# Hybrid decoder block: new leads for two products' weight slabs, their low parts by transfer in the mixers, and no forming jobs at the last convolution output

## The chip, the cores and the metric

The kernel runs on one core of a Trainium2 chip. The metric is the device time of one execution in microseconds (us); the time before is the median of three runs. In the text PE is TensorE, DVE is VectorE, ACT is ScalarE, POOL is GpSimd and SP is SyncE, as the profile names them.

## The reference

One decoder layer on x of 512 tokens by 1024 features, in float32:

```python
h = h + 0.5 * swiglu(rms_norm(h, g_ffn1), w_ffn1_gate, w_ffn1_up, w_ffn1_down)   # D_FF = 2816
z = rms_norm(h, g_mix) @ w_in                 # conv GLU | q | k | v | merge-gate logits
y_conv = conformer_conv(a_glu, w_dw, b_dw, g_conv_ln, b_conv_ln, w_conv_out)     # width 31
y_attn = o.reshape(b, s, ATTN_OUT_W) @ w_attn_out      # dilated windowed attention, 12 heads
h = h + (g_a * y_conv + g_b * y_attn) @ w_mix_out
h = h + 0.5 * swiglu(rms_norm(h, g_ffn2), w_ffn2_gate, w_ffn2_up, w_ffn2_down)
h = h + sigmoid(rms_norm(h, g_ple) @ w_ple_gate) * (p @ w_ple_proj)
return rms_norm(h, g_final)
```

swiglu(x, g, u, d) is (silu(x @ g) * (x @ u)) @ d. The change touches the product with w_mix_out ("mixers") and, through a shared table, the weights of both FFNs.

## The kernel before, in words

**Numbers in two parts.** Every matmul operand is split into a high part (the value cast to the PE's rounded 32-bit format, fp32r) and a low part (what the cast leaves out), and a product is three matmuls: high by high, high by low and low by high. A weight slab is 128 x 1024. Its high part is cast by ACT (L402, or L386). Its low part is made in one of two ways: DVE subtracts the high part from the slab (L403, in split_one); or, for a slab for which by_dma says so, ACT writes the negated cast (L372) and POOL issues a transfer that adds the slab to it in memory (L374, 512 KB), both issued by early_one, which then casts the high part too (L386).

**Seven products.** The FFNs' large steps and the mixers use a Strassen-like scheme: a step is seven products, B11, B21, T2, T1, T3, B22 and T4 (in the mixers B11, T1, T2, B22, T3, B21, T4), of sums of quarters. DVE forms the sums of the weight quarters (lines L312 to L353); the sums of the other operand come from queued jobs called forming steps (form_pair: L697 on DVE, L709 on ACT for high parts, L712 on DVE for low parts). An FFN has eleven "gate-up" steps, j = 0 to 10. Those of j = 0 and 1 are done by plain products; the others stand mostly in pairs, with "down" steps between them (PLAN). A gate-up writes its product results to three banks of the accumulator memory, PSUM: B11, T2, T3 and T4 to pa, B21 to pe, T1 and B22 to pd. ACT moves B11's, T2's and T1's result out (L999, p<-pa or p<-pd), and DVE adds the others onto these (L1012). Then come scalings by the norm (L1022), the silu of the gate (L1024), the silu behind B22 (L1026) and the products (L1027, L1004). T2, T3 and T4 are accumulated onto what pa holds, so each must wait until the state before it has been read: T3 waits for L999 of T2, and T4 for the L1012 that reads T3. Down steps and mixers add their banks to the residual on DVE (L794, L792).

**What sets the order.** Each engine works through its instructions in the order in which the program issues them, and that order comes from pointers and queues:

- The list `order` holds all slabs in order of use. For the product in use at place i, prepare() moves pointers ahead: load (SP's loads, or POOL's for the projections with w_in), sum, early (early_one) and split (split_one). soon_() moves `early` one slab at a time, and stops at slab j when j - i is over `LEAD.get(product, 9)`. It stops there whether or not that slab is one of those made early. A slab not in the table has 9. T4 has 5.
- In an FFN, jobs (the scaling and the silu of a gate among them) are issued by work(t) at the end of a product: as long as `spent`, the estimated time that ACT and DVE have been given, leaves room for the next within t (2.88 for a gate-up product). early_one, split_one and the evictions add to `spent`.
- Forming steps stand in the queue `later`. In the loop over the eight co units (the convolution's output projection, L1720 on), ten are issued behind each unit. At the last unit it is N_LAST = 3 behind the unit, then its two DVE operations (L1726, L1727), and then 10 - 3 = 7 more. In the mixers, AFTER_M gives how many forming steps follow each product: 2.

Of the kernel before, what the change touches and what calls it, by code (L numbers as in the profile page):

```python
# [22 lines left out]
KD = D // P  # L23
KF = DF // P
# [26 lines left out]

FINAL = ("B21", "T3", "B22", "T4")
HOLD = 4
LEAD = {"T4": 5, "B11": 3, "B21": 3, "T1": 3}
NEXT = 3
EARLIER = 4
FIRST = True
# [19 lines left out]
HELD = (3, 5, 7)  # L77
BY_ = False
N_FORM = 10
N_LAST = 3  # L80
AFTER_M = {"B11": 2, "T1": 2, "T2": 2, "B22": 2, "T3": 2, "B21": 2, "T4": 2}
QUOTA = {"B11": 4, "B21": 2, "T2": 1, "T1": 3, "T3": 3, "B22": 3}
POOL_MIX = False
POOL_SUMS = False
# [1 line left out]
POOLED = ("win", "v", "ao", "co")  # L86
RAISED = ("v0",)
BY_DMA = ("B11", "B21", "T4")

N_GLU = (0, 0) + (6,) * 14  # L90
N_QK = ((3, 0, 1),) * 2 + ((2, 0, 1),) * 4
# [61 lines left out]
def block_kernel(ctx: ExitStack, tc: tile.TileContext, a, out):  # L153
# [37 lines left out]
    def bank(n="ps", tag="ps"):  # L191
        return psum.tile([P, S], F32, name=name(n), tag=tag, bufs=6 if tag == "ps" else 2)
# [60 lines left out]
        return max(c.stop for _, c, _ in srcs)  # L253

    def by_dma(key):
        return (product(key) in BY_DMA and key[1:] != (("gu", KF // 2 - 1), "T4") or key[0] in POOLED + RAISED
                or key == ("2", ("dn", len(ROUNDS) - 1), "T1") or key[:2] == ("gq", "2"))

    def product(key):
        return key[2] if key[0] in ("1", "2", "m") else None  # L260
# [22 lines left out]
    def load_one(hold=False):  # L283
        i = state["load"]
        key = order[i]
        q = product(key)
        if key[0] == "gq" or q is None:
            raws[i] = fetch(sources(key), first_=key[0] in POOLED or key[0] == "gq" and by_dma(key), hold=hold)
        elif q == "B11":
            for z in (A21, A22, A11):  # L290
                quarters[key[:2], z] = fetch(quarter(key[0], key[1], z))
        elif q == (MIXED if key[0] == "m" else PRODUCTS)[1]:
            quarters[key[:2], A12] = fetch(quarter(key[0], key[1], A12))
        state["load"] = i + 1
# [70 lines left out]
    def spend(a_=0.0, v=0.0):  # L365
        spent[0] += a_
        spent[1] += v
# [8 lines left out]
    def early_one():  # L376
        i = state["early"]
        state["early"] = i + 1
        if by_dma(order[i]):
            r = raws.pop(i)  # L380
            l = W("wl", F32R)[:, :r.shape[-1]]
            if product(order[i]) or order[i][0] in RAISED:
                h = W("wh", F32R)[:, :r.shape[-1]]
                remainder(l, r, row_of([r]))
                spend(0.25 + r.shape[-1] * 0.00075)
                A.activation(h, r, AF.Copy)  # L386
            else:
                h = r
                remainder(l, h.bitcast(F32), sources(order[i]))
            halves[i] = h, l  # L390
# [36 lines left out]
    def ahead(what, one, to):  # L427
        while state[what] < min(to, len(order)):
            one()

    def soon_(i, to):

        while state["early"] < min(to + 1, len(order)):
            j = state["early"]
            lead = EARLIER if order[i][0] not in ("1", "2", "m") else NEXT
            if j - i > (LEAD.get(product(order[j]), 9) if product(order[j]) else 5 if order[j][0] == "dp" else lead):
                break
            early_one()
# [20 lines left out]
    def prepare(i, key):  # L459
# [7 lines left out]
        if state["early"] < len(order) and product(order[state["early"]]) == "T4":  # L467
            soon_(i, i + LEAD["T4"])
        ahead("load", load_one, i + ahead_ + RAW + 1 + (2 if key[0] in ("pT", "pp", "pg") else 0))
# [8 lines left out]
    def unit(ps, key, xs, ks=range(KD), beside={}):  # L478
        h, l = slab(key)
        for k in ks:  # L480
            if k in beside:
                beside[k]()
            c = slice(k * P, (k + 1) * P)
            mm3(ps, h[:, c], l[:, c], xs[k][0], xs[k][1], k == ks[0], k == ks[-1])
# [183 lines left out]
    jobs, later = [], []  # L668
# [5 lines left out]
    def next_job(queue=None):  # L674
        f, a_, v = (queue or jobs or later).pop(0)
        if queue is not later:
            spend(a_, v)
        f()
# [428 lines left out]
    def finish(norm, q):  # L1107

        if q in FINAL:
            x_, half = GOES[q]  # L1110
            for i in range(2):
                norm.add(2 * half + i, x_)
# [592 lines left out]
    for j in range(4):  # L1705
        wh, wl = slab(("ao", j))
        for i in range(2):
            m = 2 * j + i
# [11 lines left out]
    for m in range(KD):  # L1720
        p = bank("py")
        unit(p, ("co", m), cv)
        for _ in range(min(N_FORM if m < KD - 1 else N_LAST, len(later))):
            next_job(later)
        t = sg[40, m]
        V.tensor_mul(t, t, p)  # L1726
        V.tensor_add(t, t, sg.pop((48, m)))  # L1727
        if m == KD - 1:
            for _ in range(min(N_FORM - N_LAST, len(later))):
                next_job(later)  # L1730
        if m < 4:
            begun.append(form_pair(t, None, mixes[m], by=BY))
        else:
            form_pair(sg.pop((40, m - 4)), sg.pop((40, m)), mixes[m - 4], None, begun[m - 4], BY)
# [4 lines left out]
    for g in range(2):  # L1739
        ps = banks()  # L1740
        for q in MIXED:
# [13 lines left out]
            ending[:] = [lambda q=q: finish(norm, q)] if g and q in FINAL else []  # L1755
            for _ in range(min(AFTER_M.get(q, 0), len(later))):
                next_job(later)
# [184 lines left out]
```

## Time and profile before

| | |
|---|---|
| median of 3 runs | 1265.2 us (1264.93 to 1265.29) |
| profiled execution | 1265.63 us, span 1263.9 us, granted PE clock 0.999 |
| busy PE, DVE, ACT, POOL | 1252.7, 1064.7, 739.0, 232.8 us |
| pause of PE by stretch | 2.0 us in 780 to 870 (end of the co units, mixers), 0.01 in 900 to 1190 (FFN2), 7.8 in 1190 to the end |

A timeline row has the start, the duration, engine, line, operation, the tiles (written <- read), shape, count, and in brackets the idle time of the engine before it with what ended it. The page names groups of instructions by the same lines. A median from issue to landing is given for transfers.

### The profile page before, as it was taken

How to read it: one execution, taken by the hardware profiler on the slowest of the kernel's cores; microseconds unless marked ns; L12 is line 12 of the kernel's file. 1: busy time of each engine (PE TensorE's matmuls, PEld its weight loads, DVE VectorE, ACT ScalarE, POOL GpSimd, SP SyncE). 2: the span in 40 equal slices, each digit the busy share in tenths (PEclk: the TensorE clock that was granted, in tenths of full speed). 3: DMA queues.
4: the chain of work that ended last, by engine and by line, in shares of the span. 5: the costliest groups of instructions: out<-in, count | busy, mean ns of one | idle time of the engine just before them, and what ended most of it. 6: DMA issues, size and time to landing. Idle time of an engine off the chain costs nothing.

```text
span 1263.9 us, 19604 instructions
## 1 busy us (share of the span) xinstructions
PE 1252.7 (99%) x7344; PEld 1111.8 (88%) x7344; DVE 1064.7 (84%) x1714; ACT 739.0 (58%) x1078; POOL 232.8 (18%) x306
## 2 busy tenths in 40 slices
PE   9999999999999999999999999999999999999997
PEld 7898999999888889889898888878898999999886
DVE  7898898988989989898988763797589898988975
ACT  7666766665643354747565654465476766665673
POOL 0011111110222232323332222125111111110100
PEclk9999999999999999999999999999999999999999
DMA  7477778776788898988897877759668778776631
GB/s 273 111 154 203 183 178 205 165 194 164 174 193 200 188 180 185 170 180 162 174 179 177 189 167 188 195 119 272 159 153 214 159 192 204 167 172 175 167 101 67
DMA packets 121126, 222.83 MB, mean 176 GB/s; under 512 B 19128, under 2 KB 63928, under 8 KB 121032
## 3 DMA queue, kind: packets, MB, share of 16 engines
q0 software_dynamic: 47472, 139.02, 54.8%
q1 hardware_dynamic: 73128, 82.04, 20.0%
q8 instruction: 58, 0.95, 0.3%
q10 hardware_dynamic: 432, 0.52, 0.1%
q14 instruction: 36, 0.29, 0.1%
HBM read 168.56 MB, written 2.13 MB: 135 GB/s over the span
## 4 chain that ended last, share of the span: by engine, by line
PE 66%; DVE 13%; issue 9%; ACT 5%; DMA 3%; POOL 2%; SPq 0%; DVEq 0%; POOLq 0%; ACTq 0%
PE pa L768 6%; PE pa L771 5%; PE pa L769 5%; DVE acc L1250 5%; PE pa L778 3%; PE pa L779 3%; PE pa L783 3%; PE pd L768 3%; PE pd L771 3%; PE pd L769 3%; PE pd L778 1%; PE pd L779 1%; PE pd L783 1%; POOL wh L271 1%; PE pe L768 1%
## 5 line engine op out<-in xcount | busy, mean ns | idle before, releaser
L374 POOL DMA_DIRECT2D wl<-wr x92 | 78.5, 853 | 595.6 <-ACT wl L372 412.9
L1250 DVE SCALAR_TENSOR_TENSOR acc<-glu,taps,acc 128x511 f32<-128x511 f32 (+14 forms) x240 | 161.2, 731 | 0.0
L403 DVE TENSOR_TENSOR wl<-s,wh 128x1024 fp32r<-128x1024 f32 x89 | 108.5, 1219 | 30.7 <-ACT wh L402 30.7
L372 ACT ACTIVATE wl<-wh 128x1024 fp32r<-128x1024 f32 x84 | 87.7, 1052 | 77.1 <-DMA wh<-in_w_in 41.7
L402 ACT ACTIVATE wh<-s 128x1024 fp32r<-128x1024 f32 x89 | 92.5, 1050 | 40.7 <-DVE s L344 23.0
L768 PE MATMUL pa<-bh,wh 128*128 128x256 f32 x432 | 106.2, 284 | 0.0
L769 PE MATMUL pa<-bl,wh 128*128 128x256 f32 x432 | 106.0, 283 | 0.0
L372 ACT ACTIVATE wl<-wr 128x1024 fp32r<-128x1024 f32 x92 | 96.6, 1050 | 15.1 <-PE pd L779 10.0
L386 ACT ACTIVATE wh<-wr 128x1024 fp32r<-128x1024 f32 x92 | 96.2, 1045 | 0.0
L374 POOL DMA_DIRECT2D wl<-in_w_in x56 | 49.5, 884 | 222.7 <-ACT wl L372 210.5
L474 PE MATMUL pq<-xsh,wh 128*128 128x512 f32 x224 | 88.6, 396 | 0.0
L475 PE MATMUL pq<-xsl,wh 128*128 128x512 f32 x224 | 87.4, 390 | 0.0
L476 PE MATMUL pq<-xsh,wl 128*128 128x512 f32 x224 | 87.3, 390 | 0.0
L768 PEld LDWEIGHTS pa<-bh,wh 128*128 128x128 f32 x432 | 82.9, 192 | 0.4 <-ACT wh L386 0.4
L769 PEld LDWEIGHTS pa<-bl,wh 128*128 128x128 f32 x432 | 83.0, 192 | 0.0
L474 PE MATMUL pg<-xsh,wh 128*128 128x512 f32 x176 | 69.1, 392 | 0.0
L475 PE MATMUL pg<-xsl,wh 128*128 128x512 f32 x176 | 68.6, 390 | 0.1
L476 PE MATMUL pg<-xsh,wl 128*128 128x512 f32 x176 | 68.6, 390 | 0.0
L794 DVE SCALAR_TENSOR_TENSOR gx<-pa,half,gx 128x512 f32<-128x512 f32 x80 | 56.2, 745 | 8.9 <-PE pa L783 8.9
L999 ACT ACTIVATE p<-pa 128x512 f32<-128x512 f32 x36 | 21.5, 596 | 67.5 <-PE pa L771 67.1
L771 PE MATMUL pa<-bh,wl 128*128 128x256 f32 x432 | 60.7, 283 | 0.0
L771 PEld LDWEIGHTS pa<-bh,wl 128*128 128x128 f32 x432 | 55.7, 192 | 0.0
(417 smaller groups left out, 3853.6 us busy)
## 6 DMA issues: line engine op xcount, KB each, us to landing
wl<-wr POOLq DMA_DIRECT2D x92, 512.0 KB, 5.4
wh<-in_w_in POOLq DMA_DIRECT2D x56, 512.0 KB, 7.5
wl<-in_w_in POOLq DMA_DIRECT2D x56, 512.0 KB, 6.5
wr<-in_w_ffn_down SPq DMA_DIRECT2D x44, 512.0 KB, 6.3
wr<-in_w_ffn_gate SPq DMA_DIRECT2D x79, 256.0 KB, 4.8
wr<-in_w_ffn_up SPq DMA_DIRECT2D x79, 256.0 KB, 4.8
wh<-in_w_v POOLq DMA_DIRECT2D x16, 256.0 KB, 7.6
wl<-in_w_v POOLq DMA_DIRECT2D x16, 256.0 KB, 5.7
```

The costliest lines, as they stand in the source:

```text
L372: A.activation(l.bitcast(F32R), h, AF.Copy, scale=-1.0)
L374: G.dma_start(to, src, accum_op=OP.add)
L386: A.activation(h, r, AF.Copy)
L402: A.activation(h, r, AF.Copy)
L403: V.tensor_sub(l, r, h.bitcast(F32))
L474: PE.matmul(ps, wh, xh, start=start, stop=False, skip_group_check=part)
L475: PE.matmul(ps, wh, xl, start=False, stop=False, skip_group_check=part)
L476: PE.matmul(ps, wl, xh, start=False, stop=stop, skip_group_check=part)
L768: PE.matmul(o, h[:, c], th, start=q in ("B11", "B21", "T1") and i == 0, stop=False, skip_group_check=True)
L769: PE.matmul(o, h[:, c], tl, start=False, stop=False, skip_group_check=True)
L771: PE.matmul(o, l[:, c], th, start=False, stop=i >= len(at) - 2, skip_group_check=True)
L1250: bg.append(lambda acc=acc, g=g, w=w, s=s: V.scalar_tensor_tensor(acc[:, s:], g[:, :S - s], w, acc[:, s:], op0=OP.mult, op1=OP.add))
```

## The change

- LEAD has two more entries: T3 and B22 with 3, so that the pointer `early` stops in front of these slabs until they are three places ahead. The table is read for the products of both FFNs and of the mixers.
- In the mixers (keys that begin with "m") the low parts of T3 and B22 are made by ACT and a transfer, where DVE subtracted. There are two groups, so four slabs.
- At the last co unit no forming step is issued, neither behind the unit nor behind its two operations.
- Three forming steps, instead of two, follow each product of the mixers.

```diff
--- before.py
+++ after.py
@@ -51,7 +51,7 @@
 
 FINAL = ("B21", "T3", "B22", "T4")
 HOLD = 4
-LEAD = {"T4": 5, "B11": 3, "B21": 3, "T1": 3}
+LEAD = {"T4": 5, "B11": 3, "B21": 3, "T1": 3, "T3": 3, "B22": 3}
 NEXT = 3
 EARLIER = 4
 FIRST = True
@@ -77,8 +77,7 @@
 HELD = (3, 5, 7)
 BY_ = False
 N_FORM = 10
-N_LAST = 3
-AFTER_M = {"B11": 2, "T1": 2, "T2": 2, "B22": 2, "T3": 2, "B21": 2, "T4": 2}
+AFTER_M = {"B11": 3, "T1": 3, "T2": 3, "B22": 3, "T3": 3, "B21": 3, "T4": 3}
 QUOTA = {"B11": 4, "B21": 2, "T2": 1, "T1": 3, "T3": 3, "B22": 3}
 POOL_MIX = False
 POOL_SUMS = False
@@ -86,6 +85,7 @@
 POOLED = ("win", "v", "ao", "co")
 RAISED = ("v0",)
 BY_DMA = ("B11", "B21", "T4")
+M_BY_DMA = ("T3", "B22")
 
 N_GLU = (0, 0) + (6,) * 14
 N_QK = ((3, 0, 1),) * 2 + ((2, 0, 1),) * 4
@@ -253,7 +253,7 @@
         return max(c.stop for _, c, _ in srcs)
 
     def by_dma(key):
-        return (product(key) in BY_DMA and key[1:] != (("gu", KF // 2 - 1), "T4") or key[0] in POOLED + RAISED
+        return (key[0] == "m" and product(key) in M_BY_DMA or product(key) in BY_DMA and key[1:] != (("gu", KF // 2 - 1), "T4") or key[0] in POOLED + RAISED
                 or key == ("2", ("dn", len(ROUNDS) - 1), "T1") or key[:2] == ("gq", "2"))
 
     def product(key):
@@ -1720,14 +1720,11 @@
     for m in range(KD):
         p = bank("py")
         unit(p, ("co", m), cv)
-        for _ in range(min(N_FORM if m < KD - 1 else N_LAST, len(later))):
+        for _ in range(min(N_FORM if m < KD - 1 else 0, len(later))):
             next_job(later)
         t = sg[40, m]
         V.tensor_mul(t, t, p)
         V.tensor_add(t, t, sg.pop((48, m)))
-        if m == KD - 1:
-            for _ in range(min(N_FORM - N_LAST, len(later))):
-                next_job(later)
         if m < 4:
             begun.append(form_pair(t, None, mixes[m], by=BY))
         else:
```

What moves on the engines is shown at three places. PE's instructions keep their order everywhere, and so do SP's; DVE has four rows fewer (1689 for 1693), ACT and POOL four more.

ACT in one gate-up of FFN2 (j = 6), before. wh and wl with the same wr are a slab's parts; wl_10389, wh_10390 are T4's; p<-pa in row 788 is the eviction of T2, p_10375 the gate's value and L1024 its silu.

```order
783 L402 ACTIVATE wh_10385<-s_1646_10277 128x1024
784 L372 ACTIVATE wl_10389<-wr_10209 128x1024
785 L386 ACTIVATE wh_10390<-wr_10209 128x1024
786 L709 ACTIVATE bh_10425<-t_10382 128x512
787 L402 ACTIVATE wh_10428<-wr_10206 128x1024
788 L999 ACTIVATE p_10456<-pa_10350 128x512
789 L1024 ACTIVATE p_10375<-p_10375 128x512
790 L402 ACTIVATE wh_10460<-s_1652_10334 128x1024
791 L999 ACTIVATE p_10491<-pd_10466 128x512
```

The same place now, where T4's parts are wl_10432 and wh_10433 and the gate's value is p_10379:

```order
787 L402 ACTIVATE wh_10389<-s_1646_10281 128x1024
788 L1024 ACTIVATE p_10379<-p_10379 128x512
789 L709 ACTIVATE bh_10425<-t_10386 128x512
790 L402 ACTIVATE wh_10428<-wr_10210 128x1024
791 L372 ACTIVATE wl_10432<-wr_10213 128x1024
792 L386 ACTIVATE wh_10433<-wr_10213 128x1024
793 L999 ACTIVATE p_10461<-pa_10354 128x512
794 L402 ACTIVATE wh_10464<-s_1652_10338 128x1024
795 L999 ACTIVATE p_10495<-pd_10470 128x512
```

The silu L1024 has moved from behind the eviction to the place where T4's casts stood, and these stand between T3's cast L402 and the eviction. The order is like that in the gate-ups j = 3 to 9 of both FFNs. In FFN2's j = 2 the silu is ahead of the casts too; in FFN1's j = 2 it is behind the eviction of T1. At the end of FFN1's last down step the same two casts come behind a forming step L709 and an L402, instead of ahead of them.

DVE from the last co unit (L1726, L1727) into the first products of the mixers, before; L792 adds a bank to the residual.

```order
1139 L1726 TENSOR_TENSOR sg_7733<-sg_7733,py_8169 128x512
1140 L1727 TENSOR_TENSOR sg_7733<-sg_7733,sg_7316 128x512
1141 L712 TENSOR_TENSOR bl_8206<-sg_7678,bh_8205 128x512
1142 L697 TENSOR_TENSOR t_8213<-sg_7678,sg_7501 128x256
1143 L697 TENSOR_TENSOR t_8213<-sg_7678,t_8028 128x256
1144 L712 TENSOR_TENSOR b_8208<-t_8028,b_8208 128x256
1145 L712 TENSOR_TENSOR bl_8218<-t_8213,bh_8217 128x512
1146 L792 TENSOR_TENSOR gx<-gx,pa_8222 128x512
1147 L792 TENSOR_TENSOR gx<-gx,pa_8223 128x512
1148 L697 TENSOR_TENSOR t_8065<-sg_7733,t_8065 128x256
1149 L792 TENSOR_TENSOR gx<-gx,pd_8226 128x512
1150 L792 TENSOR_TENSOR gx<-gx,pd_8227 128x512
```

And now:

```order
1138 L1726 TENSOR_TENSOR sg_7733<-sg_7733,py_8169 128x512
1139 L1727 TENSOR_TENSOR sg_7733<-sg_7733,sg_7316 128x512
1140 L792 TENSOR_TENSOR gx<-gx,pa_8207 128x512
1141 L792 TENSOR_TENSOR gx<-gx,pa_8208 128x512
1142 L697 TENSOR_TENSOR t_8028<-sg_7678,t_8028 128x256
1143 L792 TENSOR_TENSOR gx<-gx,pd_8211 128x512
1144 L792 TENSOR_TENSOR gx<-gx,pd_8212 128x512
1145 L712 TENSOR_TENSOR bl_8234<-sg_7678,bh_8233 128x512
1146 L697 TENSOR_TENSOR t_8260<-sg_7678,sg_7501 128x256
1147 L697 TENSOR_TENSOR t_8260<-sg_7678,t_8028 128x256
1148 L792 TENSOR_TENSOR gx<-gx,pa_8207 128x512
1149 L792 TENSOR_TENSOR gx<-gx,pa_8208 128x512
```

The additions L792 follow the last L1727 directly, and the forming steps L697 and L712 come between and behind them.

ACT ahead of the second group's first products, before; wh_8372 is T1's high part, bh_8317 the last forming step.

```order
628 L386 ACTIVATE wh_8288<-wr_7960 128x1024
629 L372 ACTIVATE wl_8292<-wr_7956 128x1024
630 L386 ACTIVATE wh_8293<-wr_7956 128x1024
631 L709 ACTIVATE bh_8317<-t_8297 128x512
632 L372 ACTIVATE wl_8334<-wr_8178 128x1024
633 L386 ACTIVATE wh_8335<-wr_8178 128x1024
634 L402 ACTIVATE wh_8372<-s_1307_8314 128x1024
635 L402 ACTIVATE wh_8397<-s_1312_8339 128x1024
636 L402 ACTIVATE wh_8418<-s_1313_8356 128x1024
637 L402 ACTIVATE wh_8436<-wr_8174 128x1024
```

And now, where T1's high part is wh_8373:

```order
630 L709 ACTIVATE bh_8288<-t_8260 128x512
631 L709 ACTIVATE bh_8309<-sg_7733 128x512
632 L372 ACTIVATE wl_8326<-wr_8178 128x1024
633 L386 ACTIVATE wh_8327<-wr_8178 128x1024
634 L709 ACTIVATE b_8333<-t_8065 128x256
635 L709 ACTIVATE bh_8356<-t_8336 128x512
636 L402 ACTIVATE wh_8373<-s_1303_8306 128x1024
637 L402 ACTIVATE wh_8399<-s_1308_8331 128x1024
638 L372 ACTIVATE wl_8403<-s_1311_8352 128x1024
639 L386 ACTIVATE wh_8404<-s_1311_8352 128x1024
640 L372 ACTIVATE wl_8425<-wr_8174 128x1024
641 L386 ACTIVATE wh_8426<-wr_8174 128x1024
```

Two forming steps L709 that stood earlier have come to stand directly ahead of T1's cast, and the slabs of B22 (wl_8403, wh_8404) and T3 (wl_8425, wh_8426) are made by L372 and L386. On POOL, the transfer for wl_8403 now stands ahead of FFN2's first weight load (wh of w_ffn_gate), and that for wl_8425 behind it.

## The prediction

> **What bounds the kernel now.** I read the page's first part, then the busy time by stretches, then the timelines of single stretches, looking for TensorE's (PE's) pauses and for how near each wait is to becoming one.
>
> ```profile
> span 1263.9 us, 19604 instructions
> PE 1252.7 (99%) x7344; PEld 1111.8 (88%) x7344; DVE 1064.7 (84%) x1714; ACT 739.0 (58%) x1078; POOL 232.8 (18%) x306
> ```
>
> PE is busy for all but 11.2 us of the span, so nothing that relieves another engine can gain more than that, and whatever makes PE wait is added whole. The stretches say where the 11.2 us lie. The rows hold the stretch, its length, the busy time (and instructions) of PE, weight loads, DVE, ACT and POOL, the granted clock, the DMA share and GB/s.
>
> ```profile
> 780.00:870.00 90.00, 88.01 (x402) 72.33 (x401) 67.09 (x109) 45.99 (x71) 23.76 (x33) 1.00 0.79 191
> 900.00:1190.00 290.00, 289.99 (x1991) 271.11 (x1990) 252.59 (x328) 181.61 (x231) 33.82 (x40) 1.00 0.73 175
> 1260.00:1263.90 3.90, 0.00 (x0) 0.00 (x0) 0.35 (x1) 0.32 (x1) 0.00 (x0) 0.58 0.38 134
> ```
>
> The first row holds the mixers' output projection, to which the change is addressed: 1.99 us of pause, and that is the most it can gain there. The second is the body of FFN2: no pause in 290 us. A pause of no length says nothing of the cover, so I take it from the timeline of one gate-up step, whose order the change alters as well.
>
> **The side effect on the FFNs.** LEAD is read by every product of either FFN too. With T3 and B22 held to a lead of 3, the pointer of early casts stops in front of T3, and so T4's two casts (L372, L386), behind it in that order, are issued one product later. Their time counts in the budget by which queued jobs are issued; without it the budget releases the gate's silu (L1024) earlier. On ACT that turns "T4's two casts, L709, T3's cast L402, eviction L999 of T2, silu L1024" into "L1024, L709, L402, T4's two casts, L999". ACT's rows in the gate-up j = 6 of FFN2 (start, duration, in brackets an idle time before it):
>
> ```profile
> 1033.73 1.05 ACT L372 ACTIVATE wl<-wr 128x1024 fp32r<-128x1024 f32 x1
> 1034.68 1.05 ACT L386 ACTIVATE wh<-wr 128x1024 fp32r<-128x1024 f32 x1
> 1035.63 0.62 ACT L709 ACTIVATE bh<-t 128x512 fp32r<-128x512 f32 x1
> 1036.15 1.05 ACT L402 ACTIVATE wh<-wr 128x1024 fp32r<-128x1024 f32 x1
> 1037.23 0.60 ACT L999 ACTIVATE p<-pa 128x512 f32<-128x512 f32 x1
> 1037.72 0.62 ACT L1024 ACTIVATE p<-p 128x512 f32<-128x512 f32 x1
> 1038.24 1.05 ACT L402 ACTIVATE wh<-s 128x1024 fp32r<-128x1024 f32 x1
> ```
>
> DVE beside it: L1022, which makes the silu's input; L403, which needs the last L402 above; L1012, which adds T3's product out of bank pa.
>
> ```profile
> 1035.72 0.69 DVE L1022 TENSOR_TENSOR p<-p,R 128x512 f32<-128x512 f32 x1
> ...
> 1039.32 1.23 DVE L403 TENSOR_TENSOR wl<-s,wh 128x1024 fp32r<-128x1024 f32 x1 [0.26 <-ACT wh L402]
> ...
> 1044.01 0.68 DVE L1012 TENSOR_TENSOR p<-p,pa 128x512 f32<-128x512 f32 x1
> ```
>
> And PE: the first matmuls of T3 and of T4, both into bank pa. T3 needs T2's eviction (L999) out of that bank, T4 needs L1012.
>
> ```profile
> 1039.91 0.28 PE L768 MATMUL pa<-bh,wh 128*128 128x256 f32 x1
> 1045.67 0.28 PE L768 MATMUL pa<-bh,wh 128*128 128x256 f32 x1
> ```
>
> Now the eviction begins at 1037.23 and ends at 1037.83, 2.08 us before T3. After the change L1024 waits for L1022, at 1035.72 + 0.69 = 1036.41, where ACT in the row order before had other work; L709, L402, both casts and the eviction are queued behind it. From start to start these rows give 0.52 behind an L1024, 0.52 behind an L709 and 0.95 behind a cast; for an L402 I take 0.96, what the next fence leaves of its 2.01. So: L1024 1036.44, L709 1036.96, L402 1037.48, L372 1038.44, L386 1039.39, L999 1040.34 to 1040.94. T3 was due at 1039.91: PE waits 1.0 us, with its start after the eviction 1.1 us.
>
> The gate-up without casts for T4 (the last of FFN1, whose T4 is not by transfer) shows the new order already:
>
> ```profile
> 305.40 0.63 ACT L1024 ACTIVATE p<-p 128x512 f32<-128x512 f32 x1 [2.62 <-DVE p L1022]
> ...
> 307.41 0.58 ACT L999 ACTIVATE p<-pa 128x512 f32<-128x512 f32 x1
> 308.86 0.28 PE L768 MATMUL pa<-bh,wh 128*128 128x256 f32 x1
> ```
>
> There the silu does wait, for 2.62 us, and the eviction still ends at 307.99, 0.87 us before T3. Two casts of 0.95 us between them take that 0.87 and 1.03 us more: the same 1.0.
>
> A second wait follows. B22's cast L402 comes after the eviction, at 1040.83 instead of 1038.24, and DVE's L403 waits for it until 1041.90 instead of 1039.32: 2.58 us later. The rows of DVE from there to L1012 stand back to back before (4.69 us), so L1012 goes to 1046.59 and ends at 1047.27. T4, due at 1045.67 + 1.1 = 1046.77, waits for that. How soon PE follows such an addition is seen at the other gate-up, where T4 waits for it already:
>
> ```profile
> 313.96 0.68 DVE L1012 TENSOR_TENSOR p<-p,pa 128x512 f32<-128x512 f32 x1
> 314.79 0.36 PE L768 MATMUL pa<-bh,wh 128*128 128x256 f32 x1
> ```
>
> 0.15 us after its end. So T4 starts at 1047.42, 1.75 us late; with some 0.07 us to start again (a first matmul of 0.36 instead of 0.28 us) I take 1.8 us for a gate-up. DVE is then 0.8 us later against PE; the stretch row gives it 37.4 us of idle time in 290, 2.6 in the 20.15 us of a gate-up, so it catches up nearly or wholly (1.9 us for a gate-up at most). Fourteen gate-ups have these rows: the fourth to tenth of FFN1 (the first two are done plainly) and of FFN2. The third of FFN2 has another order on DVE, with more room ahead of L1012; I take the first wait alone there, 1.1 us. In FFN1's third the silu goes behind the eviction, at no cost. The sum: 14 x 1.8 + 1.1 = **26.3 us**; between 15 x 1.1 = 16.5 (only the first wait) and 15 x 1.9 = 28.5. Down steps get the casts later too, but no eviction stands behind them on ACT: nothing. The transfers that follow the casts keep their order on POOL, and SP's loads theirs; they still land in time, by the page's median from issue to landing:
>
> ```profile
> wl<-wr POOLq DMA_DIRECT2D x92, 512.0 KB, 5.4
> ```
>
> The cast at 1038.44 ends at 1039.5, and 5.4 us after that it is there, 1044.9, before T4 starts.
>
> **The end of FFN1.** The same move puts the last down step's T4 casts behind an L709 that waits for DVE, and their transfer on POOL ahead of loads for the input projection:
>
> ```profile
> 325.57 1.05 ACT L372 ACTIVATE wl<-wr 128x1024 fp32r<-128x1024 f32 x1
> 326.52 1.04 ACT L386 ACTIVATE wh<-wr 128x1024 fp32r<-128x1024 f32 x1
> 330.43 0.63 ACT L709 ACTIVATE bh<-t 128x512 fp32r<-128x512 f32 x1 [2.87 <-DVE t L697]
> 336.53 1.24 POOL L374 DMA_DIRECT2D wl<-in_w_in  x1
> 345.69 0.50 PE L476 MATMUL pa<-xsh,wl 128*128 128x512 f32 x1
> ```
>
> ```profile
> wl<-in_w_in POOLq DMA_DIRECT2D x56, 512.0 KB, 6.5
> ```
>
> L372 goes from 325.57 to 331.92 (behind L709 and one L402), its transfer to 333.3, and two loads of w_in, which were issued before 331, follow it at 333.8 and 334.4. They are what the second low part's cast waits for: with 6 to 7.5 us to land they put it at 340 to 341.3 and its transfer at 341 to 342.6, where it was issued at 336.53 before, 9.1 us ahead of its use. PE waits for it already at 345.69, being ready at 345.6. With a landing of 6.5 us, one more or less, it is there at 346.5 to 350.1: +0.9 to +4.4 us, and I take the middle, **+2.6**.
>
> **The mixers.** Four subtractions L403 leave DVE, four casts L372 and four accumulating transfers of 512 KB (POOL) come; no job stands between the last co product and the first additions, and three instead of two follow each product.
>
> ```profile
> 827.26 1.28 DVE L792 TENSOR_TENSOR gx<-gx,pa 128x512 f32<-128x512 f32 x2
> 828.09 0.47 PE L778 MATMUL pa<-wh,b 128*128 128x512 f32 x1 [1.71 <-ACT wh L402]
> 841.53 1.22 DVE L321 TENSOR_TENSOR s<-wr,s 128x1024 f32<-128x1024 f32 x1
> 844.61 0.39 PE L778 MATMUL pd<-wh,b 128*128 128x512 f32 x1
> ```
>
> T2 of the first group waits at 828.09. The profile names ACT's L402, but the bank's release counts: T2 writes pa, which the additions L792 empty, queued behind forming steps (L697, L712) until 827.26. After, they are right behind the last co addition, done by 825.5, and T2 starts at its due time 826.2. That removes 1.87 us and 0.19 within: 2.06. What is late next: in the second group an L709 on ACT waits for a subtraction on DVE that now stands behind the additions and L321 (whose row ends at 842.75 before, about a microsecond earlier now, at 841.5 with the L697 behind it ending at 841.9), and T1's cast L402 queues behind this L709: 842.4 to 843.5. T1, now due at 844.61 - 2.06 = 842.55, starts at 843.6, 1.05 us late; the additions behind it then hold T2 by 0.9 to 1.1 more. So the gain is given back: **0**, between -2.06 and +1 (a transfer that lands late by that much).
>
> **The start of FFN2.** The first load of its gate weights stands on POOL behind the new transfers of the second group:
>
> ```profile
> 839.64 1.11 POOL L271 DMA_DIRECT2D wh<-in_w_ffn_gate  x2 [2.08 <-PE pe L783]
> 853.16 2.14 POOL L374 DMA_DIRECT2D wl<-in_w_ffn_gate  x2
> 864.57 0.50 PE L476 MATMUL pu<-xsh,wl 128*128 128x512 f32 x1 [0.21 <-DMA wl<-in_w_ffn_gate]
> ```
>
> It goes from 839.64 to about 846.5, and the low part from 853.16 to 854.4 or 855; at 864.57 PE is waiting for that already. So +0 to +2.5, and I take **+1.2**, the delay of the issue.
>
> **Sum.** 26.3 + 2.6 + 0 + 1.2 = +30.1 us. The profiled execution took 1265.6, 1.7 more than its span; the median of the runs is 0.4 below it, which is nothing beside the terms. 1265.2 + 30.1 = **1295.3 us**. Against a measure of about 0.2% (2.5 us) this is slower by far.
>
> **Rivals.**
> (a) The first wait occurs, the second doesn't (DVE finds its way earlier, since PE's own wait postpones what DVE has to do): 16.5 + 3.8 = +20.3, 1285.5 us. For it: the second excess is only 0.65 us on a chain of seven instructions. Against it: that chain had no gap.
> (b) The gate-ups have the cover after all, say because the silu is not released earlier: +3.8 from the seams, 1269.0. It would need L999 to end before 1039.91, 1.0 us earlier than the row sum.
> (c) Faster or the same: FFN harmless as in (b), the transfers at the seams hidden, and the mixers keep their 2.06 us: 1263.1, which is within 0.2%. It decides when L709 of the second group is issued early enough that T1's cast ends before 842.55, and the eviction as in (b). 2.08 us of cover in the row before speak for it, and 3.9 us of new queue in front of the eviction against it.
> (d) The change doesn't do what it says: the jobs return at another place of the mixers and T2's pause remains; +2.06 on the forecast, 1297.4, inside its range.
> (e) The pauses cost clock. In the rows above the granted clock is 1.00 over 780 to 870 with a pause of 1.71 us in it, and 0.58 only in the last 3.9 us, where PE stands still. If each T3 pause let the next product (2.88 us) run at 0.58, that were 2.1 us more, 15 times: 1327 us.
>
> [...] The 1.00 beside that 1.71 us pause speaks against it, for one pause; no run here shows some 30 of them.
>
> **How the numbers follow.** Forecast with (d) 0.66, (a) 0.20, (b) 0.05, (c) 0.06 (a third of it faster by more than 0.2%), (e) 0.03. The low end takes in (a) with the mixers' gain and the seam's least: 16.5 - 2.06 + 0.9 = +15.3, 1280.5. The high end is all upper bounds: 28.5 + 4.4 + 1 + 2.5 = +36.4, 1301.6. Left out are (b), (c), (e) and little else. Faster 0.02; same 0.05 (the rest of (c) and the lower part of (b)); slower 0.93.
>
> **What would show it.** In the profile after, PE's busy time stays near 1253 us while the span grows; the stretch of FFN2 has some 14 us of pause; in a gate-up L1024 begins right at the end of L1022, T2's L999 ends a microsecond after T3 was due, T3's first matmul names it, and T4's names L1012. T2 of the first mixer has no pause, T1 of the second has. Wrong I am if the eviction L999 still ends before T3 is due: then the term of 26.3 falls whole.

## The result, and the profile after

The changed kernel takes 1302.8 us (median of 6 runs, 1301.5 to 1304.5) where the kernel before takes 1265.4 (1264.9 to 1266.5): a ratio of 1.0295, 95% interval 1.0282 to 1.0309, so 37.4 us slower. The forecast was 1295.3 us with a range of 1280.5 to 1301.6. The direction was right, and so was the mechanism of the largest term; the time lies 1.2 us above the range. The profiled execution is the slowest of the six (1304.5 us, span 1302.7), 38.8 us of span more than before.

The waits of PE after the change, as a view that groups them: who waited, for what, us in total, times, longest.

```profile
PE pa L768 <- ACT p L999: 12.8, 15, 0.9
PE pa L768 <- DVE p L1012: 4.7, 14, 0.3
PE pg L474 <- DVE xsh L502: 2.9, 1, 2.9
PE pa L476 <- DMA wl<-in_w_in: 2.3, 1, 2.3
...
PE pd L778 <- ACT wh L402: 1.0, 1, 1.0
PE pb L474 <- DVE xsl L495: 0.9, 1, 0.9
PE pa L778 <- DVE gx L792: 0.7, 1, 0.7
```

Fifteen waits for the eviction L999 and fourteen for the addition L1012 are the gate-ups, in the numbers that the prediction counted. The row for pg L474 is the start of FFN2, those for L476 and pb L474 are the input projection, and the other two the mixers. The view counts idle time alone: the 25.3 us in these rows are less than the 38.8 that the span grew, since PE's first matmul behind each wait in a gate-up took 0.38 to 0.39 us instead of 0.28, and since the clock fell, which is shown below. PE's busy time went from 1252.7 to 1267.4 us, where the prediction expected it to stay near 1253.

ACT in the same gate-up of FFN2 as in the prediction. There the whole program stands 31.34 us later by now.

```profile
1067.80 0.63 ACT L1024 ACTIVATE p<-p 128x512 f32<-128x512 f32 x1 [2.62 <-DVE p L1022]
1068.33 0.61 ACT L709 ACTIVATE bh<-t 128x512 fp32r<-128x512 f32 x1
1068.85 1.04 ACT L402 ACTIVATE wh<-wr 128x1024 fp32r<-128x1024 f32 x1
1069.80 1.04 ACT L372 ACTIVATE wl<-wr 128x1024 fp32r<-128x1024 f32 x1
1070.75 1.04 ACT L386 ACTIVATE wh<-wr 128x1024 fp32r<-128x1024 f32 x1
1071.69 0.57 ACT L999 ACTIVATE p<-pa 128x512 f32<-128x512 f32 x1
1072.17 1.05 ACT L402 ACTIVATE wh<-s 128x1024 fp32r<-128x1024 f32 x1
```

The silu begins at the end of L1022, behind 2.62 us of idle time, and the eviction five rows later. Less 31.34 these are 1036.46 and 1040.35; the prediction had 1036.44 and 1040.34. DVE's L403, which waits for the last row, and the addition L1012:

```profile
1073.25 1.23 DVE L403 TENSOR_TENSOR wl<-s,wh 128x1024 fp32r<-128x1024 f32 x1 [1.50 <-ACT wh L402]
...
1077.93 0.68 DVE L1012 TENSOR_TENSOR p<-p,pa 128x512 f32<-128x512 f32 x1
```

And the starts of T3 and T4:

```profile
1072.32 0.39 PE L768 MATMUL pa<-bh,wh 128*128 128x256 f32 x1 [0.91 <-ACT p L999]
...
1078.67 0.39 PE L768 MATMUL pa<-bh,wh 128*128 128x256 f32 x1 [0.34 <-DVE p L1012]
```

T3 starts 1.07 us late (1072.32 - 31.34 - 1039.91), T4 another 0.59 with its restart, and the next step another 0.1: 1.75 us for the gate-up.

The end of FFN1, where all is 13.1 us later. ACT's cast of the second low part, POOL's transfer for it, and PE at the first blocks of the input projection:

```profile
353.95 1.06 ACT L372 ACTIVATE wl<-wh 128x1024 fp32r<-128x1024 f32 x1 [3.79 <-DMA wh<-in_w_in]
```

```profile
355.31 0.87 POOL L374 DMA_DIRECT2D wl<-in_w_in  x1 [3.42 <-ACT wl L372]
```

```profile
358.64 0.50 PE L474 MATMUL pb<-xsh,wh 128*128 128x512 f32 x1 [0.91 <-DVE xsl L495]
...
362.32 0.80 PE L476 MATMUL pa<-xsh,wl 128*128 128x512 f32 x1 [2.27 <-DMA wl<-in_w_in]
362.92 0.63 PE L474 MATMUL pb<-xsh,wh 128*128 128x512 f32 x1
```

The cast stands at 340.8 of the old time, the transfer at 342.2 and its landing at 349.1, inside what the prediction gave for each (340 to 341.3, 341 to 342.6, 346.5 to 350.1). What it didn't have is the last row: the matmul takes 0.63 us where its like took 0.40. The stretches show why; the third number from the end is the granted clock.

```profile
361.00:369.00 8.00, 6.68 (x25) 5.85 (x26) 2.38 (x5) 2.10 (x4) 0.00 (x0) 0.57 0.73 203
887.00:891.00 4.00, 3.77 (x11) 2.95 (x11) 3.90 (x8) 2.91 (x7) 2.74 (x5) 0.57 1.14 343
920.00:1225.00 305.00, 295.61 (x1996) 272.85 (x1995) 252.35 (x328) 177.26 (x224) 32.95 (x39) 1.00 0.68 167
```

Behind the pause of 0.91 and 2.27 us the clock was at half for most of 8 us (0.50 over 362 to 368, 0.57 over the first row), and again behind the pause at the start of FFN2 (0.57 over the 4 us of the second row). Over the rest of FFN2, with fifteen of the gate-ups' waits, it was 1.00 (third row). PE paused there for 9.4 us, less than the 14 of the prediction, since of a gate-up's 1.75 us the rows above show 0.91 and 0.34 as idle time, and the rest goes with the restart (first matmuls of 0.39 us). The start of FFN2, with what ACT does ahead of it:

```profile
883.15 1.06 ACT L372 ACTIVATE wl<-wh 128x1024 fp32r<-128x1024 f32 x1 [8.62 <-DMA wh<-in_w_ffn_gate]
...
885.34 1.24 ACT L501 ACTIVATE u<-tp,gx 128x512 f32<-128x512 f32 x2
```

```profile
886.52 0.49 PE L474 MATMUL pg<-xsh,wh 128*128 128x512 f32 x1 [2.85 <-DVE xsh L502]
```

ACT waits 8.62 us for a weight load, and the norm's squares and the scaling L501, which make FFN2's input, are queued behind that cast. Last, T1 in the second group of the mixers, with the L709 that stands ahead of its cast:

```profile
861.57 0.63 ACT L709 ACTIVATE bh<-t 128x512 fp32r<-128x512 f32 x1 [5.52 <-DVE t L697]
862.10 1.99 ACT L402 ACTIVATE wh<-s 128x1024 fp32r<-128x1024 f32 x2
```

```profile
863.20 0.50 PE L778 MATMUL pd<-wh,b 128*128 128x512 f32 x1 [0.98 <-ACT wh L402]
```

The difference of matching PE starts in the two profiles, place by place:

| place | predicted | measured |
|---|---|---|
| gate-ups, FFN1 and FFN2 | 26.3 | 7 x 1.75 + 7 x 1.75 + 1.1 = 25.6 |
| late transfers in the FFNs | 0 | 0.7 (two down steps) |
| end of FFN1, input projection | 2.6 | 6.4: 3.7 at the two waits, 2.6 behind them at the lower clock |
| mixers | 0 | 1.3 |
| start of FFN2 | 1.2 | 4.1: 3.1 at the wait, the rest at the lower clock |
| start of the kernel | 0 | 0.5 |
| sum | 30.1 | 38.6 of the 38.8 us |

The half microsecond at the start of the kernel is not the change's: at the same place the profiles of the runs below lie between 0.5 us ahead of the kernel before and 0.3 us behind it.

### The profile page after: what moved, and what is told of

The parts are those of the page before. It is cut to its first block, busy times and chain, and to the rows that moved or that the text cites. A ratio compares the mean times of both kernels' runs of the same rounds, so it can differ in the third digit from the quotient of the medians.

```text
span 1302.7 us, 19608 instructions
## 1 busy us (share of the span) xinstructions
PE 1267.4 (97%) x7344; PEld 1117.4 (86%) x7344; DVE 1060.9 (81%) x1710; ACT 742.9 (57%) x1082; POOL 236.3 (18%) x310
## 5 line engine op out<-in xcount | busy, mean ns | idle before, releaser
L403 DVE TENSOR_TENSOR wl<-s,wh 128x1024 fp32r<-128x1024 f32 x87 | 106.2, 1221 | 43.3 <-ACT wh L402 43.1
L372 ACT ACTIVATE wl<-wh 128x1024 fp32r<-128x1024 f32 x84 | 87.8, 1052 | 82.8 <-DMA wh<-in_w_in 47.9
L768 PE MATMUL pa<-bh,wh 128*128 128x256 f32 x432 | 109.0, 290 | 17.5 <-ACT p L999 12.8
L372 ACT ACTIVATE wl<-wr 128x1024 fp32r<-128x1024 f32 x94 | 98.7, 1050 | 29.0 <-PE pd L779 10.0
L402 ACT ACTIVATE wh<-s 128x1024 fp32r<-128x1024 f32 x87 | 90.3, 1049 | 21.4 <-issue 10.8
L386 ACT ACTIVATE wh<-wr 128x1024 fp32r<-128x1024 f32 x94 | 98.2, 1044 | 0.0
L474 PE MATMUL pq<-xsh,wh 128*128 128x512 f32 x224 | 88.6, 396 | 0.0
L476 PE MATMUL pq<-xsh,wl 128*128 128x512 f32 x224 | 87.2, 389 | 0.0
L474 PE MATMUL pg<-xsh,wh 128*128 128x512 f32 x176 | 69.3, 394 | 2.9 <-DVE xsh L502 2.9
L476 PE MATMUL pg<-xsh,wl 128*128 128x512 f32 x176 | 68.9, 391 | 0.0
L403 DVE TENSOR_TENSOR wl<-wr,wh 128x1024 fp32r<-128x1024 f32 x30 | 36.7, 1222 | 30.9 <-ACT wh L402 30.9
L999 ACT ACTIVATE p<-pa 128x512 f32<-128x512 f32 x36 | 21.1, 586 | 61.5 <-PE pa L771 61.5
```

Of the source, the lines that this page charges most:

```text
L372: A.activation(l.bitcast(F32R), h, AF.Copy, scale=-1.0)
L403: V.tensor_sub(l, r, h.bitcast(F32))
L474: PE.matmul(ps, wh, xh, start=start, stop=False, skip_group_check=part)
L476: PE.matmul(ps, wl, xh, start=False, stop=stop, skip_group_check=part)
L768: PE.matmul(o, h[:, c], th, start=q in ("B11", "B21", "T1") and i == 0, stop=False, skip_group_check=True)
```

## The experiments

Theory L says that the loss comes from the two entries of LEAD in the FFNs; theory P that the rest comes from the new transfers on POOL, ahead of FFN2's first weights; theory G that the mixers' gain is real and is given back in the second group; theory H that a pause of PE above some 2 us costs the clock, which is 1.00 beside 1.71 us in the kernel before and 0.57 behind 2.27 and 2.85 us in the changed one. The rivals stand in the expectations.

**The new leads in the mixers alone.** In soon_ of the changed kernel:

```diff
-            if j - i > (LEAD.get(product(order[j]), 9) if ...
+            if j - i > ((9 if product(order[j]) in ("T3", "B22") and order[j][0] != "m"
+                         else LEAD.get(product(order[j]), 9)) if ...
```

> The change with its two new LEAD entries read for the mixers alone; the FFNs keep the order of before. Theory L (LEAD reorders ACT in the FFNs): the fifteen pauses at T3, those at T4 and the late start of the input projection go, 25.6 + 1.5 + 6.4 us of the 37.4. What is left is the mixers' net +1.3 and FFN2's late start, some 4.1: 1270 to 1271 us. Rival D (the four new transfers, and what they displace, make PE wait in the FFNs too): the pauses stay for the greater part, 1285 us or more. Rival M (the mixers and FFN2's start cost nothing by themselves): 1265.4 or less.

Measured: 1272.8 us against 1266.0 on that chip, ratio 1.0055 (1.0041 to 1.0069), 6.8 us slower. No wait for L999 or L1012 is left. FFN2 starts late as in the changed kernel:

```profile
866.99 0.50 PE L474 MATMUL pg<-xsh,wh 128*128 128x512 f32 x1 [2.81 <-DVE xsh L502]
```

Theory L holds, rivals D and M fall. It is some 1.5 us more than I expected; the profile has 1.1 us of it at one down step of FFN2, where a low part by transfer lands late.

**The new leads in the FFNs alone**, on the kernel before:

```diff
-            if j - i > (LEAD.get(product(order[j]), 9) if ...
+            if j - i > ((3 if product(order[j]) in ("T3", "B22") and order[j][0] != "m"
+                         else LEAD.get(product(order[j]), 9)) if ...
```

> The kernel before with T3 and B22 held to a lead of 3 in the FFNs alone; mixers as before. Theory L: the FFN's part of the loss by itself, 25.6 us at T3 and T4, about 1.5 of transfers that land late, 5 to 6.4 at the start of the input projection (with the granted clock at 0.50 for some microseconds there): 1297 to 1299 us. Rival D: 1265 to 1268 us.

Measured: 1296.9 us against 1266.0, ratio 1.0242 (1.0228 to 1.0256), 30.8 us slower, with the same waits:

```profile
PE pa L768 <- ACT p L999: 13.2, 15, 0.9
PE pa L768 <- DVE p L1012: 4.7, 14, 0.3
PE pa L476 <- DMA wl<-in_w_in: 2.2, 1, 2.2
PE pa L778 <- ACT wh L402: 1.9, 1, 1.9
```

The two parts by themselves, 30.8 and 6.8, add up to 37.6, the whole to 37.4. That the sums agree so well is in part luck, since the places differ: in this profile 1.7 us are lost at half clock (0.50 over 3.42 us) behind T2's pause in the mixers (1.87 us here), which the whole doesn't have, and 5.0 us at the input projection, where the whole loses 6.4. Four fifths of the loss come from the table's being read in the FFNs. Theory L holds.

**The forming steps alone**, on the kernel before: the two parts of the diff on N_LAST and AFTER_M.

> The kernel before with only the forming steps moved: none at the last co unit, three instead of two behind each product of the mixers; no new leads or transfers. Theory G (the gain is real and is given back in the second group, where a forming step's L709 stands ahead of T1's cast): T2's pause of 1.9 us goes, T1 and T2 of the second group pause for about 1 us each: 1265.4, within 0.7 us. Rival K (the gain is kept, and what gave it back were the transfers): 1263.3. Rival F (FFN2's late start comes from the moved steps): 1268 or more.

Measured: 1265.0 us against 1266.0, ratio 0.9992 (0.9983 to 1.0001): no difference that this shows for certain. T2's pause is gone, and T1 of the second group has one instead:

```profile
843.66 0.50 PE L778 MATMUL pd<-wh,b 128*128 128x512 f32 x1 [0.83 <-ACT wh L402]
```

In this profile PE's lead over before is 1.94 us ahead of that row, 0.95 behind it and none behind the next product. Theory G holds and rivals K and F fall: the give-back is that of the prediction, and takes no transfer.

**The transfers alone**, on the kernel before: by_dma and the leads for the mixers, with N_LAST and AFTER_M as before.

> The kernel before with only T3's and B22's low parts by transfer in the mixers (with their lead of 3 there); forming steps as before. Theory P (the transfers stand on POOL ahead of FFN2's first weights, and ACT waits for these with the norm's steps queued behind): T2's pause of 1.7 us stays, T1 of the second group has none, FFN2 starts 3 to 4.5 us late, with the clock at 0.50 if PE's pause is near 3 us: 1268.5 to 1270. Rival F (FFN2's late start comes from the forming steps): 1265 to 1266.

Measured: 1270.7 us against 1266.0, ratio 1.0038 (1.0025 to 1.0051), 4.7 us slower. T2's pause stays (1.72 us), and ACT waits for FFN2's weights with the norm's steps behind:

```profile
862.58 1.06 ACT L372 ACTIVATE wl<-wh 128x1024 fp32r<-128x1024 f32 x1 [7.21 <-DMA wh<-in_w_ffn_gate]
```

Theory P holds and rival F falls: the late start of FFN2 comes from the transfers. How they make the load late is not separated, their place ahead of it on POOL or their traffic: from issue to landing FFN2's first loads of high parts took a median of 6.9 us in the kernel before (836 to 866 us) and 9.8 us in the changed kernel (858 to 888 us). Another 1.6 us of this profile are lost at a down step of FFN2, the one that lost 1.1 us with the leads in the mixers alone.

**The silu held behind the eviction**, with the leads in the FFNs alone:

```diff
                     t[q] = T("p")
                     A.activation(t[q], p, AF.Copy)
                     spend(0.63)
+                    if q == "T2" and "held" in t:
+                        while jobs:
+                            next_job()
+                        t["gate"] = t.pop("held")
+                        A.activation(t["gate"], t["gate"], AF.Silu)
+                        spend(0.63)
...
-                    if q == "B21":
+                    if q == "B21" and j < KF // 2 - 1:
+                        t["held"] = z
+                    elif q == "B21":
                         job(lambda z=z: (A.activation(z, z, AF.Silu), t.update(gate=z)), 0.63)
```

> The kernel with the FFN's new leads alone (the casts of T4 one product later), but the silu of the gate is issued behind T2's eviction, where it stood before, in all gate-ups but the last of each FFN. Theory S (the pauses come from the silu: it waits for DVE's L1022 with the eviction queued behind it): both pauses of the gate-ups go, and what is left are the late start of the input projection (about 5 us with the clock's part) and transfers landing late, 0.5 to 2: 1271 to 1273 us. Rival C (the two casts ahead of the eviction are enough): the pauses stay and it is 1290 or more.

Measured: 1272.0 us against 1265.5, ratio 1.0053 (1.0039 to 1.0066), and no wait in any gate-up. ACT has T4's casts a product late and the eviction on time (the silu's line is L1005 here):

```profile
1040.38 1.05 ACT L372 ACTIVATE wl<-wr 128x1024 fp32r<-128x1024 f32 x1
1041.33 1.05 ACT L386 ACTIVATE wh<-wr 128x1024 fp32r<-128x1024 f32 x1
1042.41 0.60 ACT L999 ACTIVATE p<-pa 128x512 f32<-128x512 f32 x1
1042.90 0.62 ACT L1005 ACTIVATE p<-p 128x512 f32<-128x512 f32 x1
```

So the 25 us are not the price of later casts. They are that of one instruction, issued 2.6 us before its input is ready and ahead of four others. Theory S holds and rival C falls.

**The same, with the last down step of FFN1 left as before:**

```diff
-            if j - i > ((3 if product(order[j]) in ("T3", "B22") and order[j][0] != "m"
+            if j - i > ((3 if product(order[j]) in ("T3", "B22") and order[j][0] != "m"
+                         and order[j][:2] != ("1", ("dn", len(ROUNDS) - 1))
```

> As the run with the silu held, and in the last down step of FFN1 the leads of before, so that T4's casts stand there as before. Theory S and B (the late start of the input projection comes from these two casts alone): 1266 to 1268 us, with no pause at the first two blocks of the input projection and a granted clock of 1.00 there. Rival (the start is late because of the casts in the gate-ups before): as the run before, 1271 or more.

Measured: 1266.4 us against 1265.5, ratio 1.0010 (1.0001 to 1.0019); the run before and this one differ by 5.6 us, the whole late start. Theory S and B holds, and its rival falls. One of the ten executions took 1271.4 us; the profile is of one that took 1265.4 and doesn't show why. The stretch at the input projection has its clock again:

```profile
340.00:350.00 10.00, 9.81 (x60) 8.19 (x59) 6.36 (x11) 6.86 (x13) 1.41 (x2) 1.00 0.97 247
```

**Forming steps spread otherwise:** as with the forming steps alone, but

```diff
-AFTER_M = {"B11": 3, "T1": 3, "T2": 3, "B22": 3, "T3": 3, "B21": 3, "T4": 3}
+AFTER_M = {"B11": 2, "T1": 4, "T2": 5, "B22": 5, "T3": 4, "B21": 2, "T4": 2}
```

> The kernel before with no forming step at the last co unit, but with 2, 4, 5, 5, 4, 2, 2 forming steps behind the mixers' products instead of 3 each, so that the last L709 does not have to wait behind the additions and L321 on DVE. No new leads or transfers. Theory G (the give-back is that one L709 ahead of T1's cast): T2's pause goes and T1's and T2's pauses in the second group stay away: 1.5 to 2 us under the kernel before, 1263.5 to 1264.5 on a chip where that takes 1266. Rival (any order of these steps makes some addition wait): within 0.5 us of the kernel before.

Measured: 1265.2 us against 1265.5, ratio 0.9999 (0.9990 to 1.0008). The rival is right here: the pause at T1 of the second group is gone, but 0.6 us appear at T4 of the first group (for an L709) and 0.6 at T2 of the second (for L792).

**That, with transfers in the first group alone:**

```diff
-        return (product(key) in BY_DMA and ...
+        return (key[:2] == ("m", ("mx", 0)) and product(key) in ("T3", "B22") or product(key) in BY_DMA and ...
```

and the lead of 3 for these two products of that group.

> The spread forming steps of the run before (none at the last co unit; 2, 4, 5, 5, 4, 2, 2 behind the mixers' products), and T3's and B22's low parts by transfer in the first group of the mixers alone, with the lead of 3 there. The second group and the FFNs keep the order of before. Theory V (the mixers are bound by DVE, which works without a gap there, so PE's pause comes back later unless DVE loses work, here two subtractions of 1.2 us; FFN2's loads on POOL are not behind the new transfers): the 2.1 us of T2's pause are kept for the greater part, 1.5 to 2 us faster than before, FFN2's start in time. Rival (FFN2's start is held by the DMA traffic of any new transfer): 1 us slower than before or more.

Measured: 1265.1 us against 1266.0, ratio 0.9994 (0.9985 to 1.0003): not told from no change. The mixers' stretch of the kernel before and of this one (DVE's busy time is the third of the pairs):

```profile
820.00:853.00 33.00, 31.29 (x138) 25.44 (x137) 32.57 (x48) 20.52 (x24) 7.00 (x11) 1.00 0.54 126
```

```profile
820.00:853.00 33.00, 32.81 (x145) 26.72 (x144) 31.75 (x48) 22.68 (x28) 9.71 (x14) 1.00 0.77 166
```

Before, DVE is busy for 32.57 of 33 us, so the pause of PE that was taken away at T2 of the first group came back where DVE was late: 0.83 us at T1 of the second with the forming steps alone, 0.6 us at each of two places with them spread. With two subtractions less, PE is busy for 32.81 instead of 31.29: 1.5 us are kept at the mixers, and FFN2 starts in time. Of these, 0.7 us are lost again in this profile at the down step of FFN2 named above. The median is 0.9 us lower, of which the interval leaves open whether it is anything; the 1.5 to 2 us that theory V expected did not come.

**The price of a pause.** Idle activations on ACT ahead of FFN2's first block, on the kernel before, K = 4, 8 and 12 of them:

```diff
+    def pause():
+        z = T("idle")
+        for _ in range(K):
+            A.activation(z[:, :KD * TAPS], taps, AF.Copy)
...
-                    (lambda: over(xs, V_G2, low, us2)) if g and q == "T4" else None)
+                    (lambda: (pause(), over(xs, V_G2, low, us2))) if g and q == "T4" else None)
```

> The kernel before with 4 idle activations of 128x248 on ACT (0.3 us each from start to start) put ahead of the first scaled block of FFN2's input, so that PE pauses for some 1.2 us at that place. Nothing else is changed. Theory H (a pause of PE costs its own length up to about 2 us, and more only above it, where the granted clock falls to 0.50 for several microseconds): clock 1.00, 1.0 to 1.3 us slower than before. Rival W (the clock fell at the seams for another reason, such as the DMA traffic there): the same here, and no fall with 8 or 12 either.

> As the run before with 8 activations: a pause of some 2.5 us. Theory H: this is near the edge; the clock may fall in some executions, 2.5 us slower without and 4 with. Rival W: 2.5 us slower and a clock of 1.00.

> As the run before with 12 activations: a pause of some 3.7 us. Theory H: the clock falls to 0.50 for three to seven microseconds behind the pause, and the loss is 3.7 plus 1.3 to 3, 5 to 7 us. Rival W: 3.7 us slower and a clock of 1.00.

Measured: 1266.6, 1269.5 and 1271.5 us against 1265.9; ratios 1.0005 (0.9996 to 1.0014), 1.0030 (1.0018 to 1.0041) and 1.0047 (1.0032 to 1.0062). For each, PE's pause and the stretch behind it. K = 4:

```profile
864.18 0.49 PE L474 MATMUL pg<-xsh,wh 128*128 128x512 f32 x1 [1.16 <-DVE xsh L502]
```

```profile
863.00:868.00 5.00, 3.61 (x18) 2.78 (x18) 4.20 (x8) 4.57 (x10) 2.91 (x5) 1.00 1.13 328
```

K = 8:

```profile
865.64 0.55 PE L474 MATMUL pg<-xsh,wh 128*128 128x512 f32 x1 [2.82 <-DVE xsh L502]
```

```profile
865.00:870.00 5.00, 4.18 (x11) 3.11 (x12) 4.71 (x9) 4.03 (x9) 3.05 (x4) 0.66 1.12 290
```

K = 12:

```profile
867.76 0.80 PE L474 MATMUL pg<-xsh,wh 128*128 128x512 f32 x1 [4.75 <-DVE xsh L502]
```

```profile
866.00:874.00 8.00, 6.24 (x18) 4.68 (x19) 5.50 (x10) 5.11 (x11) 2.86 (x4) 0.57 1.14 289
```

With 1.2 us the clock stayed at 1.00 beside the same DMA traffic (the column behind it, 1.13), with 2.8 and 4.7 us it fell (0.66 over 5 us, 0.57 over 8). The pauses came out longer than I had aimed at (4.7 instead of 3.7 for K = 12), so the times have to be held against the pauses measured: 0.7, 3.6 and 5.6 us of loss for 1.2, 2.8 and 4.7 us. Rival W falls. Theory H holds in that the longer pauses (2.8 and 4.7 us) cost the clock here and the short one (1.2 us) didn't; its edge, about 2 us, is too high, since 1.87 us cost it too, as the last section shows.

## Why the prediction missed by a little

Two steps of the sum failed, the end of FFN1 and the start of FFN2: 3.8 us were forecast for both together, 6.9 at their upper bounds, and 10.5 were measured. Both left out the half clock behind the pause, and the second followed the wrong path. That the miss is small is luck in part, since the gate-ups came out 2.9 us below their own upper bound.

**Right.** The step "the side effect on the FFNs" holds in each part: 25.6 us measured for 26.3, with the starts of the silu and the eviction to 0.02 us, T3 for L999, T4 for L1012, fourteen gate-ups and one that lacks the second wait; the runs with the leads in one place alone and with the silu held show that this is the cause. Rivals (a) to (d) fell. The mixers' gain and its give-back came as worked out, and the run with the forming steps alone shows them by themselves.

**Wrong: "the end of FFN1", +2.6.** The chain of casts and transfers was right row for row and put the landing between +0.9 and +4.4; with 3.7 us for both waits it was near the upper end, since the input's own blocks were late too (0.91 us for L495): ACT makes them behind the cast that waits 3.79 us for a load of w_in. But the term ended with the wait. The 2.6 us behind it, at a clock of 0.50 (362 to 368), were in no bound.

**Wrong: "the start of FFN2", +1.2, bound +2.5.** I took the delay of the low part's issue, because PE waits for that part in the profile before. The path ran elsewhere: the late load of the high part holds ACT at L372, the norm's L661 and L501 stand behind it, and PE waits for the input. ACT's idle time at that cast was 3.83 us before and 8.62 after, and the run with the transfers alone loses 3.9 us there, against 4.1. The wait came to 3.1 us, and the half clock behind it (0.50 over 3.4 us) added 1.0. ACT's timeline of the kernel before shows that path, and I hadn't followed it:

```profile
859.00 1.06 ACT L372 ACTIVATE wl<-wh 128x1024 fp32r<-128x1024 f32 x1 [3.83 <-DMA wh<-in_w_ffn_gate]
...
861.20 1.25 ACT L501 ACTIVATE u<-tp,gx 128x512 f32<-128x512 f32 x2
```

**Wrong in place: rival (e), 0.03.** I priced the clock on the gate-ups, where the pauses are short, and gave it up on the strength of one pause of 1.71 us. There it was right to: the clock is 1.00 over the 305 us of FFN2 with its fifteen waits, each 0.9 us or less. The clock fell at the two other pauses that the prediction itself had, with 2.6 and 1.2 us; they measured about 3 us each (0.91 and 2.27 us, with a clock of 0.57 behind them over 8 us, and 2.85 us, with 0.57 over 4).

**Mis-sized: the mixers, 0, bound +1.** Measured +1.3; the part beyond is at B21 of the second group, whose low part lands late (0.4 us of idle time in PE's row, 0.7 by the starts of its matmuls). That the transfers in the FFNs "still land in time" was off by 0.7 us. Late landings at the down step of FFN2 cost 0.4 to 1.6 us in the four profiles that have new transfers in the mixers, 0.3 us in that with the leads in the FFNs alone and nothing in the others. How transfers in the mixers reach a place 270 us later was not settled.

## What to carry to other kernels

A table that is read by name is read by everybody who uses the name: list what else moves, and look first at the engine with the least slack, not at the place that the change is about. An instruction that is issued sooner than its input is ready can do harm by all that stands behind it on its engine: here the silu waited for 2.62 us on ACT, and the eviction behind it came at 1040.35 instead of 1037.23. The price can be read from the rows by adding start to start. When a sum has a pause of PE in it as long as those that cost the clock here (1.87 us and more), add the clock's part to it, as a bound at least: half of the 3.4 or 6.8 us that the clock was 0.50 here, 1.7 or 3.4 us.

## What the runs showed of the hardware

In these profiles the half clock came in pieces of one length. From the rows above, (1 - clock) x 2 x length of the stretch is 3.4 us behind the pause of 2.8 us (0.66 over 5 us), 6.9 behind that of 4.7 (0.57 over 8 us), 6.9 at the input projection after the change (0.57 over 8) and 3.4 at the start of FFN2 (0.57 over 4).

A pause of less than 2 us was enough once. With the leads in the FFNs alone, T2's pause in the mixers is 1.87 us, and the clock falls behind it, with no DMA traffic beside it. The stretches below have the length of one such piece, 3.41 us, and are counted from where the half clock begins:

```profile
845.59 0.47 PE L778 MATMUL pa<-wh,b 128*128 128x512 f32 x1 [1.87 <-ACT wh L402]
```

```profile
842.96:846.37 3.41, 1.54 (x7) 0.87 (x6) 3.05 (x8) 2.10 (x3) 0.00 (x0) 1.00 0.00 0
846.37:849.79 3.42, 3.42 (x9) 2.66 (x9) 2.94 (x5) 3.38 (x5) 0.77 (x1) 0.50 0.00 0
```

With K = 8 the same pause is 1.73 us, and lies within one such stretch too; the clock stays:

```profile
825.00:828.41 3.41, 1.68 (x8) 1.06 (x7) 3.05 (x7) 2.10 (x3) 0.00 (x0) 1.00 0.00 1
828.41:831.82 3.41, 3.41 (x16) 2.71 (x15) 3.41 (x7) 2.93 (x4) 0.32 (x1) 1.00 0.00 0
```

In the changed kernel, at the input projection, PE was idle for another 0.72 us within the first piece (361.60 to 365.01), and with K = 12 for 1.18 us (866.58 to 869.99); in both a second piece followed. With K = 8 it was 0.18 us (865.96 to 869.37), at the start of FFN2 none (887.25 to 890.66), and the clock was back at 1.00 behind the one piece.

The half clock began 0.7 us behind the end of the pause at FFN2's start (887.25 for 886.52), but 1.2 us ahead of it with K = 12 (866.58 for 867.76). So 1.73 us of pause at T2 of the mixers left the clock at 1.00, and 1.87 us cost it 3.4 us at 0.50. What else decides it, and whether 1.87 us would cost it at another place, was not shown: no run moved a pause of one length.
